# When the loads and splits of one bias matrix run, and which engine scales and shifts the first norm, in a one-layer hybrid decoder kernel

## The chip, the cores and the metric

The kernel runs as one program on one core of a Trainium2 chip. The metric is device microseconds of one execution, from launch to end. The kernel before was run three times: median 1319.92 us, from 1318.84 to 1320.48.

## The reference

One decoder layer for 256 tokens of width 1024, all in float32, with the batch of one:

```python
mod = silu(c) @ ada_w + ada_b                  # shift, scale and gate of two sub-layers
h   = rmsnorm(x, norm1_g) * (1.0 + sc1) + sh1
x   = x + g1 * hybrid_mixer(h)                 # attention and mLSTM from one projection of h
h   = rmsnorm(x, norm2_g) * (1.0 + sc2) + sh2
x   = x + g2 * routed_moe(h)                   # 4 of 32 experts per token
return rmsnorm(x, final_g)
```

`hybrid_mixer` projects h with one wide matrix, runs stick-breaking attention over 16 heads of 64 and an mLSTM over 4 heads of 256, gates the two results and projects them back. Each expert computes `clamped_swiglu(xb @ w1 + b1) @ w2 + b2`; `b1` is a 32 x 2048 matrix of biases, one row per expert. It is this `b1` that the change is about, and the line with `sh1` and `sc1`.

## The kernel before, in words

x lies transposed in SBUF, as `xT`: 128 partitions of features, eight blocks `kt` of 256 tokens. The program has four stages.

1. **Start.** Small loads, silu of c (`silr`), the mean square of x by eight matmuls against a constant matrix (`rms_T`, line 202), and from it 1/rms, `rs1`, by a Ln and an Exp on ScalarE (`rsqrt_of`, lines 223 and 224).
2. **First stage, eight blocks kt** (lines 337 to 385). For each block `start_h` loads 1 MB of `ada_w` and reduces it against `silr` on VectorE (line 187, two instructions, giving shift and scale of the block), forms `A1` (line 361), and makes h: x times rs1 (line 359), times A1 plus shift (line 362), both on VectorE; a rounded copy `hhi` on ScalarE (line 363); and the rest `hlo` on VectorE (line 364). `start_w` loads 0.9 MB of projection weights, in two pieces of 1024 and 768 columns for each partition, and splits them likewise: `yahi` or `ybhi` on ScalarE (line 347), `yalo` or `yblo` on VectorE (line 348). `start_c` issues 45 matmuls of 128x256 on TensorE (lines 375 and 378) that accumulate seven projected chunks and the two gate rows. Weights go through a ring of four wide slots, each of which holds one block's ada piece and weight piece; a slot is loaded again when both pieces are used up.
3. **The rest of the mixer** (lines 488 to 700): four chunks of attention, each in two halves (line 515 onward), with softplus and exponential work on ScalarE and VectorE between matmuls; then the mLSTM by heads (`conv`, `scores`, `read_out`, `finish`), the gates and the output projection. Each further chunk of weights is loaded (line 113), split into `whi` (ScalarE, line 238) and `wlo` (VectorE, line 240) and used by 48 matmuls (lines 274 to 276 and 303 to 305). Pieces of `ada_w` for the later shifts are reduced in between (line 187 again).
4. **Experts**: 16 pairs of experts, whose weights stream through the rings; at the start of a pair one small matmul per bank adds `b1` (line 951).

For that matmul `b1` is kept as `b1s`, three bf16 parts of the same matrix on the partitions 0 to 127. Four groups g of 512 columns are made one after the other: four loads from the POOL queue into one tile `bt` (line 476), a rounded copy on ScalarE (line 480), and twice a subtraction on VectorE (line 482) followed by a copy on ScalarE (line 483). The tile `bt` has a single buffer:

```python
def load_b1(g):
    bts[g] = mx.tile([128, 512], F32, name="bt", bufs=1)
    for i in range(4):
        nc.gpsimd.dma_start(bts[g][32 * i:32 * i + 32], a["b1"][:, 512 * g:512 * g + 512])
```

What sets the order of the work: the program is written stage by stage, but the framework arranges the instructions of each engine by priorities and estimates of its own. Each engine then runs its list strictly in that order, and so does each DMA queue (SP's for most loads, POOL's for `b1` and a few small ones). An instruction that has to wait holds everything behind it on its engine. `tc.issue_after(x)` keeps what is issued under it behind instruction x in the arranged order. The calls of `step_of_b1` stand in the loops of the attention and of the mLSTM (lines 554 and 657), with no such tie, and the arranged lists have the `b1` work much earlier, between the instructions of the first stage.

Of the kernel before, what the change touches and what calls it, by code (L numbers as in the profile page):

```python
# [13 lines left out]
F32 = mybir.dt.float32  # L14
# [4 lines left out]
AF = mybir.ActivationFunctionType  # L19
OP = mybir.AluOpType  # L20
# [3 lines left out]
T = 256  # L24
D = 1024
KT = 8
# [37 lines left out]
def body(tc, a, out):  # L64
    nc = tc.nc
    mm = nc.tensor.matmul
    act = nc.scalar.activation
# [131 lines left out]
    def mod_of(m, kt):  # L199
        return modT[:, 8 * m + kt:8 * m + kt + 1]  # L200
# [123 lines left out]
    pif = ps_m.tile([128, 512], F32, name="pm")  # L324
    first.append(ps_m.tile([128, 512], F32, name="pm").rearrange("p (n t) -> p n t", n=2))
    wf, parts = {}, {}
    order, his = [], []
    wi = mx.tile([128, KT, 64], F32, name="cv")
    nc.gpsimd.memset(wi, 0.0)
    nc.gpsimd.tensor_copy(wi[:, :, 0:4], wif[:, :, 0:4])  # L330
    nc.gpsimd.tensor_copy(wi[:, :, 32:36], wif[:, :, 4:8])
    wihi, wilo = (mx.tile([128, KT, 64], F32R, name="cs") for _ in range(2))
    with tc.issue_after(rs1_ins):
        act(wihi, wi, AF.Copy)
    tt(wilo, wi, f32(wihi), OP.subtract)

    def start_w(kt):
        w = wf[kt] = next_slot([128, 1792])
        if kt:
            nc.sync.dma_start(w, a["w_first"][kt])  # L340
        else:
            for b in (slice(0, 1024), slice(1024, 1792)):
                nc.sync.dma_start(w[:, b], a["w_first"][kt][:, b])
        hi, lo = ((yahi, yalo), (ybhi, yblo))[kt % 2]
        for b in (slice(0, 1024), slice(1024, 1792)):
            x, h, l = (t[:, b] for t in (w, hi.rearrange("p a b -> p (a b)"), lo.rearrange("p a b -> p (a b)")))
            act(h, x, AF.Copy)
            tt(l, x, f32(h), OP.subtract)
        parts[kt] = hi, lo

    def start_h(kt):
        wa = next_slot([128, 2, D])
        if 0 < kt < KT - 1:
            nc.sync.dma_start(wa, a["ada_1"][kt])
        else:
            for i in range(2):
                nc.sync.dma_start(wa[:, i], a["ada_1"][kt][:, i])
        t0 = mx.tile([128, T], F32, name="sq")
        tt(t0, xT[:, kt, :], rs1, OP.mult)
        ada(wa, 0, (kt, 8 + kt))  # L360
        stt(A1[:, kt:kt + 1], modT[:, 8 + kt:9 + kt], 1.0, col[:, C_N1 + kt:C_N1 + kt + 1], OP.add, OP.mult)
        ts(t0, t0, A1[:, kt:kt + 1], mod_of(SH1, kt), op0=OP.mult, op1=OP.add)
        his.append(act(hhi[:, kt, :], t0, AF.Copy).ins)
        tt(hlo[:, kt, :], t0, f32(hhi)[:, kt, :], OP.subtract)

    def start_c(kt):
        hi, lo = parts[kt]
# [103 lines left out]
    bts = {}  # L471

    def load_b1(g):
        bts[g] = mx.tile([128, 512], F32, name="bt", bufs=1)
        for i in range(4):
            nc.gpsimd.dma_start(bts[g][32 * i:32 * i + 32], a["b1"][:, 512 * g:512 * g + 512])

# [7 lines left out]
    def step_of_b1(g):  # L485
        if g:
            split_b1(g - 1)
        if g < 4:
            load_b1(g)

    for c in range(4):
        if c > 2:
            qs[c] = mx.tile([128, 2, T], F32, name="q")
            pq = proj_T(take(), hT)
            fetch()
            act(qs[c], pq, AF.Copy, scale=0.125)
        q = qs[c]
        if c > 1:
            pk = proj_T(take(), hT)
            fetch()  # L500
        else:
            pk = first[1 + 4 * c]
        nc.vector.tensor_copy(kp[0:64, :, 0, :], pk[0:64])
        nc.vector.tensor_copy(kp[64:128, :, 1, :], pk[64:128])
        if c > 1:
            pv = proj_N(take())
            fetch()
            v = mx.tile([128, 2, 256], F32, name="v")
            act(v, pv, AF.Copy)
        else:  # L510
            v = vs[c]
        py = ps_m.tile([128, 512], F32, name="pm").rearrange("p (n t) -> p n t", n=2)
        for n in range(2):

            z = ps_z.tile([128, 2, 512], F32, name="pz").rearrange("p a b -> p (a b)")
            for s in range(2):
                for h in range(2):
                    o = z[:, 256 * h:256 * h + 256] if s == 0 else z[:, 512 + 128 * h:640 + 128 * h]
                    mm(o, kp[:, n, h, 128 * s:128 * s + 128], q[:, n, 128 * s:], start=h == 0, stop=False,
                       skip_group_check=True)  # L520
                o = z[:, 512 * s:512 * s + 512 - 256 * s].rearrange("p (h t) -> p h t", h=2)
                mm(o[:, :, 0:128], identb, nm1[:, None, :].to_broadcast([128, 2, 128]), start=False, stop=s == 1,
                   skip_group_check=True)
            zz = z[:, 0:768]
            l = mx.tile([128, 768], F32, name="l")
            act(l, zz, AF.Abs)
            act(l, l, AF.Exp, scale=-1.0)
            act(l, l, AF.Ln, bias=1.0)
            sp = mx.tile([128, 768], F32, name="sp")
            stt(sp, zz, 0.0, l, OP.max, OP.add)  # L530
            hi = mx.tile([128, 768], F32R, name="so", bufs=1)
            lo = mx.tile([128, 768], F32R, name="sp")
            act(hi, sp, AF.Copy)
            nc.vector.tensor_tensor(lo, sp, f32(hi), OP.subtract)
            late_q = z[:, 0:512].rearrange("p (h t) -> p h t", h=2)[:, :, 128:256]
            for x in (hi, lo):
                last = x is lo
                mm(late_q, sums[:, 1], x[:, 512:768], start=False, stop=False, skip_group_check=True)
                mm(z[:, 0:512], sums[:, 0], x[:, 0:512], start=False, stop=last, skip_group_check=True)
                mm(z[:, 512:768], sums[:, 0], x[:, 512:768], start=False, stop=last, skip_group_check=True)  # L540
            e = mx.tile([128, 768], F32, name="l")
            act(e, zz, AF.Exp)
            for h in range(2):
                hs = slice(64 * (2 * n + h), 64 * (2 * n + h) + 64)
                o = py[64 * h:64 * h + 64, n, :]
                mm(o, v[:, 0, hs], e[:, 256 * h:256 * h + 256], start=True, stop=False, skip_group_check=True)
                mm(o[:, 128:256], v[:, 1, hs], e[:, 512 + 128 * h:640 + 128 * h], start=False, stop=True,
                   skip_group_check=True)
        act(yahi[:, 2 * c:2 * c + 2, :], py, AF.Copy)
        tt(yalo[:, 2 * c:2 * c + 2, :], py, f32(yahi)[:, 2 * c:2 * c + 2, :], OP.subtract)  # L550
        if c == 0:
            split_M()
        if c in {1: 0, 2: 1, 3: 2}:
            step_of_b1({1: 0, 2: 1, 3: 2}[c])
        later((0,0,1,3,)[c])


# [95 lines left out]
    for hd in range(4):  # L653
        S, so = scores(hd, *qk[hd], last)
        later((2,2,2,2,)[hd])
        if hd in {0: 3, 1: 4}:
            step_of_b1({0: 3, 1: 4}[hd])
        if hd < 3:
            qk[hd + 1] = qk_of(hd + 1)
        last = hd, read_out(hd, S), so  # L660
# [604 lines left out]
```

## Time and profile before

| what | us |
|---|---|
| median of three runs | 1319.92 |
| lowest and highest | 1318.84, 1320.48 |
| the profiled execution, device time | 1320.84 |
| its span, from first to last instruction | 1319.2 |

Busy time over the span, by engine: TensorE (PE) 1224.6 us or 93%, VectorE (DVE) 467.9 us or 35%, ScalarE (ACT) 330.8 us or 25%, GpSimd (POOL) 32.3 us or 2%. The sixteen DMA engines moved 483.41 MB, 366 GB/s on average.

To read it: the averages mix stages that have different limits, so the stages are read one by one. A row of a timeline gives the start, the duration (or, where xN is larger than one, the time that the group of N took), engine, line, operation, output and inputs; a bracket gives the idle time of the engine just ahead and what ended it. Matmuls of one engine overlap, so the pace of TensorE is the distance between two starts, not the duration of one row. PEclk or "granted clock" is the share of full speed that TensorE was given: 1.00 is 2.4 GHz, 0.50 is 1.2 GHz.

### The profile page before, as it was taken

The numbers are of one execution on the slowest core, as the hardware profiler recorded it, in microseconds if no ns is written. First come the engines' busy times: TensorE is split into PE (matmuls) and PEld (weight loads), VectorE is DVE, ScalarE is ACT, GpSimd is POOL, SyncE is SP. The second block draws the span as 40 slices with busy tenths as digits, with TensorE's granted clock in tenths as the row PEclk, the third lists the DMA queues.
The fourth block names the chain that finished last, engine by engine and source line by source line (L and its number), as shares of the span: only waits on it lengthen the run. The fifth ranks groups of instructions, "written<-read, shape, count | busy, mean of one in ns | idle before, by whom it ended". The sixth has DMA issues, their size and how long they took to land. (4 is left out here: it accounts for less than half of the span.)

```text
span 1319.2 us, 16510 instructions
## 1 busy us (share of the span) xinstructions
PE 1224.6 (93%) x6859; PEld 675.7 (51%) x6874; DVE 467.9 (35%) x923; ACT 330.8 (25%) x616; POOL 32.3 (2%) x63
## 2 busy tenths in 40 slices
PE   4989999999989999999999999989887999989887
PEld 3978999999963343344433344333333333333333
DVE  4968898786530222031211212112012112112013
ACT  3557767655521110101101011010101011010102
POOL 3100000000000000000000000000000000000002
PEclk7989999999989999998999999999999999999999
DMA  9675556496669899999999999999999999999995
GB/s 337 216 269 223 225 209 258 173 382 241 256 225 418 354 416 428 427 426 426 428 428 426 429 427 427 427 426 427 428 426 425 426 427 427 427 428 428 427 423 212
DMA packets 44989, 483.41 MB, mean 366 GB/s; under 512 B 5318, under 2 KB 6742, under 8 KB 10860
## 3 DMA queue, kind: packets, MB, share of 16 engines
q1 hardware_dynamic: 43740, 480.53, 88.0%
q0 software_dynamic: 624, 1.23, 0.3%
q8 instruction: 56, 0.92, 0.3%
q10 hardware_dynamic: 544, 0.52, 0.1%
q14 instruction: 25, 0.20, 0.0%
HBM read 481.21 MB, written 1.05 MB: 366 GB/s over the span
## 5 line engine op out<-in xcount | busy, mean ns | idle before, releaser
L823 PE MATMUL s<-w,xg 128*64 128x512 f32 x2032 | 465.2, 601 | 30.3 <-DMA w<-in_w 27.0
L823 PEld LDWEIGHTS s<-w,xg 128*64 128x64 f32 x2032 | 135.6, 137 | 298.8 <-issue 244.7
L823 PE MATMUL t<-w,whi 128*64 128x512 f32 x948 | 212.3, 596 | 11.7 <-ACT whi L874 9.6
L840 DVE SCALAR_TENSOR_TENSOR xT<-pm,modT,xT 128x256 f32<-128x256 f32 x128 | 56.0, 480 | 391.3 <-PE pm L823 391.3
L823 PEld LDWEIGHTS t<-w,whi 128*64 128x64 f32 x948 | 65.1, 137 | 137.1 <-issue 114.0
L240 DVE TENSOR_TENSOR wlo<-w,whi 128x512 fp32r<-128x512 f32 x164 | 110.1, 687 | 43.3 <-ACT whi L238 42.7
L858 ACT ACTIVATE wlo<-wlo 128x512 f32<-128x512 f32 x32 | 20.1, 629 | 417.8 <-DVE wlo L856 411.5
L238 ACT ACTIVATE whi<-w 128x512 fp32r<-128x512 f32 x162 | 100.9, 630 | 83.9 <-PE pj L275 65.9
L856 DVE TENSOR_SCALAR wlo<-s 128x512 f32<-128x512 f32 x32 | 22.1, 691 | 238.6 <-PE s L823 223.5
L274 PE MATMUL pj<-hhi,whi 128*128 128x256 f32 x368 | 105.0, 285 | 1.5 <-ACT sgate L685 1.1
L276 PE MATMUL pj<-hhi,wlo 128*128 128x256 f32 x368 | 105.1, 286 | 0.5 <-DVE wlo L240 0.5
L275 PE MATMUL pj<-hlo,whi 128*128 128x256 f32 x368 | 104.4, 284 | 0.0
L274 PEld LDWEIGHTS pj<-hhi,whi 128*128 128x128 f32 x368 | 70.5, 192 | 2.5 <-ACT sgate L685 1.3
L276 PEld LDWEIGHTS pj<-hhi,wlo 128*128 128x128 f32 x368 | 70.4, 191 | 1.5 <-DVE wlo L240 1.1
L275 PEld LDWEIGHTS pj<-hlo,whi 128*128 128x128 f32 x368 | 70.5, 191 | 0.2 <-issue 0.2
L823 PEld LDWEIGHTS pm<-G,mghi 128*128 128x128 f32 x512 | 59.5, 193 | 17.9 <-issue 17.3
L823 PE MATMUL pm<-S,whi 128*128 128x256 f32 x240 | 67.3, 404 | 0.2 <-DVE xT L840 0.2
L823 PEld LDWEIGHTS pm<-S,whi 128*128 128x128 f32 x240 | 40.8, 189 | 50.0 <-issue 34.6
L823 PE MATMUL pm<-G,mghi 128*128 128x128 f32 x512 | 63.8, 280 | 0.2 <-ACT xg L851 0.2
L187 DVE CUSTOM_DVE_ANT_0 w<-w,silr,col 128x1024 f32<-128x1024 f32 x48 | 60.3, 1279 | 1.0 <-ACT silr L673 0.5
L874 ACT ACTIVATE whi<-pm 128x512 f32<-128x512 f32 x32 | 19.1, 597 | 162.2 <-PE pm L826 162.2
L851 ACT ACTIVATE xg<-pm,modT 128x128 f32<-128x128 f32 x128 | 37.1, 368 | 69.4 <-PE pm L823 69.4
(367 smaller groups left out, 1300.9 us busy)
## 6 DMA issues: line engine op xcount, KB each, us to landing
w<-in_w SPq DMA_DIRECT2D x176, 2048.0 KB, 32.6
w<-in_w_in SPq DMA_DIRECT2D x29, 1024.0 KB, 8.1
w<-in_ada SPq DMA_DIRECT2D x22, 1024.0 KB, 7.0
w<-in_w SPq DMA_DIRECT2D x20, 1024.0 KB, 8.5
w<-in_w_first SPq DMA_DIRECT2D x7, 896.0 KB, 9.9
w<-in_w_last SPq DMA_DIRECT2D x6, 1024.0 KB, 34.4
w<-in_w_a SPq DMA_DIRECT2D x4, 1024.0 KB, 7.7
w<-in_w_b SPq DMA_DIRECT2D x4, 1024.0 KB, 13.2
```

The source lines that it names most:

```text
L187: nc.vector.tensor_tensor_reduce(out=w[:, j + n, :], in0=w[:, j + n, :], in1=SILU[-1], scale=1.0, scalar=col[:, C_AB + i:C_AB + i + 1], op ...
L238: act(hi, x, AF.Copy)
L240: nc.vector.tensor_tensor(lo, x, f32(hi), OP.subtract)
L274: mm(ps[:, n, :], whi[:, j, s], mhi[:, kt, :], start=kt + n == 0, stop=False, skip_group_check=True)
L275: mm(ps[:, n, :], whi[:, j, s], mlo[:, kt, :], start=False, stop=False, skip_group_check=True)
L276: mm(ps[:, n, :], wlo[:, j, s], mhi[:, kt, :], start=False, stop=last, skip_group_check=True)
L823: return tc.keep_in_program_order(mm(*args, **kw))
L840: stt(xT[:, kt, :], p[:, j, :], mod_of(G2, kt), xT[:, kt, :], OP.mult, OP.add)
L851: act(xg[kt] if isinstance(xg, list) else xg[:, kt, :], p[:, width * j:width * j + width], AF.Identity, bias=mod_of(SH2, kt))
L856: ts(g, glu, LIMIT, None, op0=OP.min)
L858: act(s, g, AF.Sigmoid, scale=ALPHA)
L874: act(aT[hf], pt.rearrange("p (k m) -> p k m", k=4), AF.Copy)
```

## The change

The loads and splits of `b1` are tied to the attention: in each chunk c they are kept behind the two instructions that end the chunk, step c after chunk c, and the last split (step 4) is in the first head of the mLSTM. Their tile takes a buffer of `cs` (two buffers, used also by the gate rows, by the sigmoid in `conv` and by `hn`) in place of the one of `bt`.

Scale and shift of the first norm move to ScalarE: `hhi` is written by an ACTIVATE with the scale and the shift as operands, and a second ACTIVATE of the same inputs writes the unrounded h that `hlo` needs. The VectorE instruction of line 362 is gone. x times rs1 is made for 1, 2, 3 and 2 blocks at once into tiles of the attention that are not yet in use.

Besides, the second piece of the first block's weight split is kept behind rs1 and behind the first x times rs1, and the split of the gate weights (`wihi`, `wilo`) is kept behind the first h.

```diff
+    def split_if(ins):
+        with tc.issue_after(ins):
+            act(wihi, wi, AF.Copy)
+        tt(wilo, wi, f32(wihi), OP.subtract)
...
+            if kt == 0 and b.start:
+                with tc.issue_after(rs1_ins), tc.issue_after(first_t0):
+                    act(h, x, AF.Copy)
+                    tt(l, x, f32(h), OP.subtract)
+                continue
...
+    def normed1(kt):
+        for k0, n, name, at in ((0, 1, "sp", 0), (1, 2, "sp", 1), (3, 3, "sp", 0), (6, 2, "so", 0)):
+            if k0 <= kt < k0 + n:
+                if k0 not in x1:
+                    x1[k0] = (x1[0] if at else mx.tile([128, 768], F32, name=name, bufs=2 if name == "sp" else 1)
+                              .rearrange("p (k t) -> p k t", k=3))
+                    made.append(tt(x1[k0][:, at:at + n], xT[:, k0:k0 + n],
+                                   rs1[:, None, :].to_broadcast([128, n, T]), OP.mult).ins)
+                return x1[k0], at + kt - k0
...
-        t0 = mx.tile([128, T], F32, name="sq")
-        tt(t0, xT[:, kt, :], rs1, OP.mult)
         ada(wa, 0, (kt, 8 + kt))
         stt(A1[:, kt:kt + 1], modT[:, 8 + kt:9 + kt], 1.0, col[:, C_N1 + kt:C_N1 + kt + 1], OP.add, OP.mult)
-        ts(t0, t0, A1[:, kt:kt + 1], mod_of(SH1, kt), op0=OP.mult, op1=OP.add)
-        his.append(act(hhi[:, kt, :], t0, AF.Copy).ins)
-        tt(hlo[:, kt, :], t0, f32(hhi)[:, kt, :], OP.subtract)
+        x, k = normed1(kt)
+        h = mx.tile([128, T], F32, name="sq")
+        act(hhi[:, kt, :], x[:, k, :], AF.Identity, scale=A1[:, kt:kt + 1], bias=mod_of(SH1, kt))
+        h_ins = act(h, x[:, k, :], AF.Identity, scale=A1[:, kt:kt + 1], bias=mod_of(SH1, kt)).ins
+        tt(hlo[:, kt, :], h, f32(hhi)[:, kt, :], OP.subtract)
+        if kt == 0:
+            split_if(h_ins)
+        if kt < KT - 1:
+            normed1(kt + 1)
...
-        bts[g] = mx.tile([128, 512], F32, name="bt", bufs=1)
+        bts[g] = mx.tile([128, 512], F32, name="cs")
...
-        act(yahi[:, 2 * c:2 * c + 2, :], py, AF.Copy)
-        tt(yalo[:, 2 * c:2 * c + 2, :], py, f32(yahi)[:, 2 * c:2 * c + 2, :], OP.subtract)
+        on_act = act(yahi[:, 2 * c:2 * c + 2, :], py, AF.Copy).ins
+        on_dve = tt(yalo[:, 2 * c:2 * c + 2, :], py, f32(yahi)[:, 2 * c:2 * c + 2, :], OP.subtract).ins
         if c == 0:
             split_M()
-        if c in {1: 0, 2: 1, 3: 2}:
-            step_of_b1({1: 0, 2: 1, 3: 2}[c])
+        with tc.issue_after(on_act), tc.issue_after(on_dve):
+            step_of_b1(c)
...
-        if hd in {0: 3, 1: 4}:
-            step_of_b1({0: 3, 1: 4}[hd])
+        if hd == 0:
+            step_of_b1(4)
```

What it does to the arranged lists is shown at three places. The first is ScalarE's list between the table load that precedes 1/rms and the first block of h. Before (`b1s<-bt` is a step of `b1`, `yahi<-w` a weight split, `rs` is 1/rms, `cs<-cv` the gate weights):

```order
L163 ACT_TABLE_LOAD
L480 ACTIVATE b1s<-bt 128x512
L347 ACTIVATE yahi<-w 128x1024
L223 ACTIVATE rs<-pm,epsc 128x256
L347 ACTIVATE yahi<-w 128x768
L224 ACTIVATE rs<-rs 128x256
L334 ACTIVATE cs<-cv 128x512
L483 ACTIVATE b1s<-bt 64x512
L363 ACTIVATE hhi<-sq 128x256
```

and with the change:

```order
L163 ACT_TABLE_LOAD
L353 ACTIVATE yahi<-w 128x1024
L223 ACTIVATE rs<-pm,epsc 128x256
L224 ACTIVATE rs<-rs 128x256
L350 ACTIVATE yahi<-w 128x768
L385 ACTIVATE hhi<-sp,modT,A_162 128x256
L386 ACTIVATE sq<-sp,modT,A_162 128x256
L335 ACTIVATE cs<-cv 128x512
```

The two `b1s` rows have left this stretch, and the second weight piece and the gate weights stand behind 1/rms and behind h.

The second place is VectorE's list at the end of the first stage, from the scale of the last block to the copies of k (`kp`) that the first attention matmuls read. Before:

```order
L361 SCALAR_TENSOR_TENSOR A_162<-modT,col 128x1
L406 CAST sums<-cst 128x128
L362 TENSOR_SCALAR sq<-sq,A_162,modT 128x256
L409 CAST nm<-sq 128x256
L418 COPY bf<-bif 4x1
L439 CAST neg_698<-l 68x512
L364 TENSOR_TENSOR hlo<-sq,hhi 128x256
L425 MEMSET sq 4x256
L482 TENSOR_TENSOR bt<-bt,b1s 64x512
L482 TENSOR_TENSOR bt<-bt,b1s 32x512
L503 COPY kp<-pz 64x2x256
L504 COPY kp<-pz 64x2x256
```

and with the change:

```order
L382 SCALAR_TENSOR_TENSOR A_162<-modT,col 128x1
L433 CAST sums<-cst 128x128
L445 COPY bf<-bif 4x1
L466 CAST neg_697<-l 68x512
L387 TENSOR_TENSOR hlo<-sq,hhi 128x256
L452 MEMSET sq 4x256
L530 COPY kp<-pz 64x2x256
L531 COPY kp<-pz 64x2x256
L436 CAST nm<-sq 128x256
```

The scale and shift (`sq<-sq,A`) and the two `bt` rows are gone ahead of `kp`, and the cast of the mask `nm` stands behind it.

The third place is ScalarE's list with the change, at the end of the last attention chunk (names with their numbers, so that the groups of `b1` can be told apart: `cs_866`, `cs_1372` and `cs_1092` are the groups 1, 3 and 2):

```order
L510 ACTIVATE b1s_721<-cs_866 32x512
L238 ACTIVATE whi_1528<-w_1442 128x512
L569 ACTIVATE l_1330<-pz_1307 128x768
L553 ACTIVATE l_1343<-pz_1336 128x768
L238 ACTIVATE whi_1532<-w_1442 128x512
L554 ACTIVATE l_1343<-l_1343 128x768
L238 ACTIVATE whi_1536<-w_1442 128x512
L555 ACTIVATE l_1343<-l_1343 128x768
L596 ACTIVATE xpad1_1388<-pj_1474 128x2x256
L238 ACTIVATE whi_1605<-w_1603 128x512
L507 ACTIVATE b1s_721<-cs_1372 128x512
L560 ACTIVATE so_1349<-sp_1347 128x768
```

Between the last copy of group 1 and the first copy of group 3, which takes its buffer, now stand nine rows; the four loads of group 3 can start only after that last copy, on the POOL queue, where nothing else stands ahead of them. Further on in the same list the sigmoids of the first head's q and k stand on both sides of a table load, so this head has four table loads where it had two.

## Rows read from the trace of the kernel before

**Rows 1.** Windows: stretch, length, PE, PEld, DVE, ACT, POOL busy, PEclk, DMA share, GB/s.

```profile
27.50:62.50 35.00, 35.00 (x272) 34.92 (x272) 34.70 (x63) 16.67 (x24) 3.91 (x8) 0.92 0.72 258
...
80.00:160.00 80.00, 78.31 (x576) 70.31 (x577) 67.91 (x113) 61.01 (x96) 0.00 (x0) 0.96 0.56 214
...
160.00:280.00 120.00, 117.27 (x938) 114.31 (x937) 106.69 (x215) 79.78 (x136) 3.88 (x4) 1.00 0.62 245
...
400.00:1200.00 800.00, 755.78 (x3569) 294.25 (x3584) 148.68 (x315) 91.15 (x217) 3.81 (x13) 0.99 1.00 423
```

**Rows 2.** Timeline of ScalarE, 21 to 28 us: start, time, instruction, idle ahead.

```profile
21.77 0.63 ACT L480 ACTIVATE b1s<-bt 128x512 bf16<-128x512 f32 x1 [9.52 <-DMA bt<-in_b]
...
22.31 1.04 ACT L347 ACTIVATE yahi<-w 128x1024 fp32r<-128x1024 f32 x1
...
23.26 0.46 ACT L223 ACTIVATE rs<-pm,epsc 128x256 f32<-128x256 f32 x1
...
24.35 0.40 ACT L224 ACTIVATE rs<-rs 128x256 f32<-128x256 f32 x1
...
27.03 0.42 ACT L363 ACTIVATE hhi<-sq 128x256 fp32r<-128x256 f32 x1 [1.12 <-DVE sq L362]
```

**Rows 3.** Timeline of SP's queue: issue of the first block's weight pieces.

```profile
3.49 1.00 SPq L343 DMA_DIRECT2D w<-in_w_first  x2
```

**Rows 4.** DMA issues, 0 to 80 us: count, KB each, us to landing.

```profile
w<-in_w_first SPq DMA_DIRECT2D x1, 512.0 KB, 11.4
```

**Rows 5.** Timeline of VectorE: first block's weight split and x times 1/rms.

```profile
23.38 1.22 DVE L348 TENSOR_TENSOR yalo<-w,yahi 128x1024 fp32r<-128x1024 f32 x1
...
24.78 0.43 DVE L359 TENSOR_TENSOR sq<-xT,rs 128x256 f32<-128x256 f32 x1 [0.17 <-ACT rs L224]
```

**Rows 6.** Timeline of TensorE: the first stage's first matmul.

```profile
27.50 0.58 PE L375 MATMUL pz<-hhi,yahi 128*128 128x256 f32 x1 [13.70 <-ACT hhi L363]
```

**Rows 7.** Windows of TensorE: stretch, length, busy (matmuls), PEclk, DMA share, GB/s.

```profile
28.00:30.00 2.00, 2.00 (x11) 0.50 1.00 394
```

**Rows 8.** Groups of VectorE, 27.5 to 62.5 us: count, busy us, mean ns.

```profile
L482 DVE TENSOR_TENSOR bt<-bt,b1s 32x512 f32<-32x512 f32 (+1 forms) x4 | 2.8, 689 | 0.1
...
L362 DVE TENSOR_SCALAR sq<-sq,A,modT 128x256 f32<-128x256 f32 x6 | 2.5, 413 | 0.2
```

**Rows 9.** Timeline of TensorE from the eighth block to the attention.

```profile
70.47 0.58 PE L375 MATMUL pz<-hhi,ybhi 128*128 128x256 f32 x1 [2.16 <-ACT hhi L363]
...
73.62 0.39 PE L375 MATMUL pz<-hlo,ybhi 128*128 128x256 f32 x1
73.84 0.29 PE L375 MATMUL pz<-hhi,yblo 128*128 128x256 f32 x1
73.96 0.28 PE L375 MATMUL pz<-ybhi,hlo 128*128 128x256 f32 x1
...
81.45 2.05 PE L519 MATMUL pz<-q,kp 128*128 128x256 f32 x4 [3.87 <-DVE kp L504]
...
87.42 0.40 PE L274 MATMUL pj<-hhi,whi 128*128 128x256 f32 x1
...
96.66 1.13 PE L519 MATMUL pz<-q,kp 128*128 128x256 f32 x4
...
98.21 0.36 PE L305 MATMUL pj<-whi,hlo 128*128 128x256 f32 x1
```

**Rows 10.** Timeline of ScalarE: the last step of `b1` that waits for its load.

```profile
77.13 0.63 ACT L480 ACTIVATE b1s<-bt 128x512 bf16<-128x512 f32 x1 [6.71 <-DMA bt<-in_b]
```

**Rows 11.** The tile `bt`: its loads, from issue to landing.

```profile
DMA to landing us min/median/max: 3.9/5.3/9.5
```

**Rows 12.** Timeline of ScalarE: a table load and its neighbours.

```profile
153.89 0.60 ACT L549 ACTIVATE yahi<-pm 128x512 fp32r<-128x512 f32 x1 [0.47 <-PE pm L547]
154.51 1.28 ACT L578 ACT_TABLE_LOAD   x1
155.80 0.63 ACT L578 ACTIVATE cs<-cv 128x512 f32<-128x512 f32 x1
```

More of the change, by code (lines that the diff above doesn't have):

```diff
@@ L326, in body @@
     wf, parts = {}, {}
-    order, his = [], []
+    order = []
     wi = mx.tile([128, KT, 64], F32, name="cv")
@@ L332, in body @@
     wihi, wilo = (mx.tile([128, KT, 64], F32R, name="cs") for _ in range(2))
-    with tc.issue_after(rs1_ins):
-        act(wihi, wi, AF.Copy)
-    tt(wilo, wi, f32(wihi), OP.subtract)
+    def split_if(ins):
+        with tc.issue_after(ins):
+            act(wihi, wi, AF.Copy)
+        tt(wilo, wi, f32(wihi), OP.subtract)
     def start_w(kt):
@@ L349, in start_w @@
         parts[kt] = hi, lo
+    x1 = {}
+    def normed1(kt):
[7 more added lines that the diff above has]
+                return x1[k0], at + kt - k0
+    made = []
+    normed1(0)
+    first_t0 = made[0]
     def start_h(kt):
```

## The prediction

> **What bounds the kernel now.** I read the windows first, because the averages mix stages. Of the 35 us from 27.5 on, which are six blocks of the first stage, TensorE is busy for 35.00 and VectorE for 34.70 at a granted clock of 0.92 [rows 1]: both are full. From 80 to 160 us, in the attention, TensorE has 78.31 of 80, VectorE 67.91 and ScalarE 61.01; from 160 to 280 TensorE still has 117.27 of 120. So the mixer is paced by TensorE, with VectorE close behind. In the experts (400 to 1200) the DMA share is 1.00 at 423 GB/s, while in the three mixer windows it is 0.72, 0.56 and 0.62. The experts' loads start when TensorE gives slots free in the mixer, and the DMA engines have room there, so I expect an earlier end of the mixer to pass on in full.
>
> Then the timelines, for places where TensorE does nothing. There are three. The first matmul of the stage starts at 27.50 after 13.70 us of idleness, which an `hhi` of ScalarE ends [rows 6]. The eighth block starts at 70.47 after 2.16 us, again for `hhi`, and the attention starts at 81.45 after 3.87 us, for a `kp` copy of VectorE [rows 9]. Behind each the clock is low: from 28 to 30 us it is 0.50, the lower of its two levels, 1.2 GHz, against 2.4 [rows 7]; after 70.47 the starts are 0.22 us apart (73.62 to 73.84) until they fall to 0.12 (73.84 to 73.96) [rows 9].
>
> What holds the first is in ScalarE's timeline: the first split of `b1` stands ahead of everything and waits 9.52 us for its load, until 21.77 [rows 2]. The same wait, 6.71 us until 77.13, comes back at the end of the stage [rows 10]; behind it VectorE's last steps of `b1` stand ahead of `kp`, as the second place of the arranged lists shows.
>
> **The change part by part.**
>
> *The start.* With the `b1` row gone, ScalarE's first work is the weight split. Its piece of 512 KB is issued by SP at 3.49 [rows 3] and lands 11.4 us later [rows 4], at 14.9. The mean square is no later than that: before, TensorE is done with it at 27.50 − 13.70 = 13.80 [rows 6]. Then, on ScalarE, `yahi` 1.04 (15.9), Ln 0.46 and Exp 0.40 (16.8) [rows 2]; on VectorE beside it `yalo` 1.22 (17.1), then x times 1/rms 0.43 (17.5) [rows 5]; then `hhi` 0.42 [rows 2], 18.0. The second weight piece waits on purpose until that chain is through. With a hand-over of 0.1 the first matmul starts at 18.1 instead of 27.50: **−9.4**. Bounds: a w_first load 3 us later, since loads that were spread now crowd, gives −6.4; nothing gives more than −10.
>
> *The six blocks.* VectorE loses the scale and shift, 2.5 us in six or 0.41 for each block, and the `b1` subtractions, four of 0.69 or 0.46 for each block [rows 8]. From 34.70/6 = 5.8 us a block it falls to 4.9. TensorE needs 45 matmuls at 0.12, 5.4. So TensorE becomes the slower and VectorE runs ahead of it. ScalarE gets a second copy of h per block, 0.42 to 0.60 us as the rows for 256 and 512 columns bound it [rows 2, 12]; it was busy for 16.67 of 35 [rows 1], so that costs nothing while its wait for `b1` is gone. x times 1/rms for several blocks moves the same elements in fewer instructions: nothing. The gain is at the eighth block: the idle 2.16 goes, and so do the slow matmuls between 70.47 and 73.84, some 3.37/0.22 = 15 of them at 0.10 too much, 1.5. Together **−3.7**. Lower bound 0, if the eighth block's ada load and not VectorE makes it late; upper −6, if VectorE cost further time in earlier blocks.
>
> *The gap ahead of the attention.* `kp` now follows `hlo` directly in VectorE's list. The 3.87 shrink to 0.3, about a copy's time: **−3.6**, between −2.5 and −3.9.
>
> *The first attention matmuls.* After the gap they run from 81.45 to 87.42, 5.97 us for two half chunks' worth of four; a later group of four takes 98.21 − 96.66 = 1.55 at full clock [rows 9], two of them 3.1. Without a gap the clock stays up: **−2.9**; 0 if the work then waits for other engines.
>
> *What is given back.* The `b1` work moves to where TensorE is paced by its own work, but the others are nearly full: twelve ScalarE instructions of 0.63 [rows 10], 7.5 us, and eight of VectorE of 0.69 [rows 8], 5.5 us, against 19 us that ScalarE and 12.1 that VectorE have free in the 80 us [rows 1]. The first head also gets two more table loads of 1.28 [rows 12], 2.6 us of ScalarE. If all is hidden, 0. If none of VectorE's is and the table loads show in full, 8.1; and a late group of `b1` can add to it: the load of group 3 waits for group 1's last copy, takes up to 9.5 us [rows 11], and ScalarE has nine instructions of about 0.60 [rows 12], 5.4, to fill that time, so it stands for up to 4.1. That makes 12.2 in all. I take **+3**, nearer to hidden: TensorE's idle time in that window is 1.7 of 80 with VectorE at 85%; I let it double, +1.7, and half of the table loads show, +1.3. Below 0 I see nothing, since no wait is removed there.
>
> On the table loads the Trainium skill speaks against the change: "ScalarE: Activation LUTs", section "What ACT_TABLE_LOAD costs", puts a switch at about 2.66 us, a load of 1.28 and a drain of about 1.38. The trace agrees on the load, 1.28, and shows no drain: the neighbours end at 154.49 and start at 155.80 around a load from 154.51 to 155.79 [rows 12]. By the page the two loads would be 5.3, and the sum 1.4 higher.
>
> **The sum** goes against the profiled execution, 1320.84, which is 0.92 above the median of the three: 1320.84 − 9.4 − 3.7 − 3.6 − 2.9 + 3.0 = 1304.2, and 0.92 less on the median's scale, 1303.3, rounded to **1303.0**.
>
> **The rivals.**
>
> *The attention gives back more.* The bounds above, taken together: the `b1` steps show as waits of TensorE, the last group's load holds ScalarE, and each halt is followed by matmuls at the low clock. For it: VectorE has only 12.1 us free of 80, and the steps sit at the ends of chunks, where the next chunk's weights are split. Against it: they are tied behind the chunk's own last instructions, and the scores for the next half stand ahead. A give-back of 8 to 12 makes 1308 to 1312. Chance 0.16.
>
> A rule of the Trainium skill would feed this rival: "SBUF — State Buffer", section "SBUF: two separate sides", says that a load issued by POOL waits for its descriptors while VectorE runs certain copies. The trace so far speaks against a large effect: with VectorE busy for 34.70 of 35 us [rows 1], loads of `bt` issued by POOL landed within 9.5 us at most [rows 11].
>
> *The first stage becomes bound by its loads.* A block takes 1.92 MB; at the 258 GB/s of the window [rows 1] that is 7.4 us against TensorE's 5.4. If the four blocks that have to wait for a slot of the ring came at that pace, 8 us would be lost again: about 1311. Against it: the 258 is what was asked for, not what can be had; the DMA share is 0.72, and from 28 to 30 us 394 GB/s flow [rows 7], which is 4.9 us a block. Chance 0.06.
>
> *The gain does not arrive.* The experts are bound by DMA with share 1.00 [rows 1]; if their loads start no earlier, whatever the mixer gains is a wait at the first pair: 1320, the same. Against it: DMA shares of 0.56 to 0.72 in the mixer. Chance 0.04.
>
> *Slower.* ScalarE and VectorE become the bound in the attention: in each of the eight half chunks TensorE waits and then runs at the low clock, as it did at 70.47, where a wait of 2.16 brought 1.5 of slow matmuls, 3.66 together [rows 9]. All eight would be 29.3, against 19.6 gained: about 1329. It decides from the sixth of the eight on. For it: 67.91 and 61.01 of 80 us [rows 1] get 5.5 and 10.1 us more, 92 and 89%. Against it: neither passes 100%. Chance 0.03.
>
> **How the numbers follow.** The forecast has 0.71, its own range 1299 to 1308: a give-back from 0 to 8 makes 1300.3 to 1308.3, and the upper bounds of stage and gap reach some 1.3 further down. The start's −6.4 and the stage's 0 lie within the same spread. The range for 8 in 10 takes in most of the first rival: 1298.5 to 1310.5. A measurement of this kernel can tell about 0.2%, 2.6 us, from no change. Faster by more: the forecast and the first two rivals, 0.93. Within it: 0.04. Slower: 0.03.
>
> **What would show it.** In the timeline of TensorE the first stage starts near 18 and no idle time over 0.5 us stands ahead of the eighth block or the attention, which starts near 64.7 (81.45 − 9.4 − 3.7 − 3.6), at a granted clock of 1.00. ScalarE has no wait for `b1` ahead of the first h. VectorE is under 90% busy in the first stage. From the attention's start to its end TensorE's idle time is under 4 us; if it is over 8, the first rival holds. ScalarE's row for group 3's first copy shows whether it waits for its load. If the first stage's blocks wait for `w` or `ada` loads, the second rival holds; if the first pair of experts starts as early as the mixer ends but its weights come late, the third. The prediction is wrong if the start of the attention moves by less than 15 us, or if it moves and the end doesn't.

## The result, and the profile after

With the change the kernel takes 1301.42 us (median of four runs, 1300.57 to 1303.24), against 1319.38 for the kernel before in four runs beside it. The ratio is 0.9863, with a 95% interval from 0.9847 to 0.9878: 18 us faster. The profiled execution took 1301.86 us, its span is 1300.2 against 1319.2 before. The forecast was 1303.0. One slow execution of the kernel before (2487 us) and one of the ninth kernel below (2825 us) are in no time or ratio given.

The windows of the kernel with the change, cut at stretches that answer to [rows 1] (length, busy time and number of instructions of PE, PEld, DVE, ACT and POOL, granted clock, DMA share, GB/s):

```profile
18.00:53.00 35.00, 35.00 (x276) 35.00 (x275) 33.28 (x54) 18.63 (x27) 0.00 (x0) 0.93 0.96 378
62.00:142.00 80.00, 78.68 (x603) 71.05 (x602) 72.28 (x120) 62.34 (x101) 7.88 (x16) 1.00 0.67 244
...
400.00:1200.00 800.00, 753.45 (x3565) 292.03 (x3576) 154.61 (x327) 90.57 (x214) 3.82 (x13) 1.00 1.00 423
```

The experts look as before, 423 GB/s at a DMA share of 1.00; they only begin earlier. In the attention (second row) VectorE has 4.4 us more work in 80 than it had, ScalarE 1.3. In the first stage VectorE is still busy for 33.28 of 35 us, which the prediction had not expected.

ScalarE's timeline at the start (start, time, instruction, idle time ahead) shows the wait for `b1`, 9.52 us in [rows 2], gone; it waits 1.98 us for the weights instead, and the chain down to `hhi` runs through:

```profile
13.92 1.06 ACT L353 ACTIVATE yahi<-w 128x1024 fp32r<-128x1024 f32 x1 [1.98 <-DMA w<-in_w_first]
14.88 0.46 ACT L223 ACTIVATE rs<-pm,epsc 128x256 f32<-128x256 f32 x1
15.37 0.42 ACT L224 ACTIVATE rs<-rs 128x256 f32<-128x256 f32 x1
15.69 0.83 ACT L350 ACTIVATE yahi<-w 128x768 fp32r<-128x768 f32 x1
16.60 0.60 ACT L385 ACTIVATE hhi<-sp,modT,A 128x256 fp32r<-128x256 f32 x1
```

TensorE's timeline at the places that answer to [rows 6, 9], the eighth block among them (57.85), and each later place in the mixer down to the gates where it stood idle for 0.3 us or more:

```profile
17.26 0.58 PE L402 MATMUL pz<-hhi,yahi 128*128 128x256 f32 x1 [3.33 <-ACT hhi L385]
...
57.54 0.28 PE L405 MATMUL pm<-hhi,cs 128*64 128x256 f32 x1
57.85 0.39 PE L402 MATMUL pz<-hhi,ybhi 128*128 128x256 f32 x1
...
63.35 1.02 PE L546 MATMUL pz<-q,kp 128*128 128x256 f32 x4
...
66.33 0.36 PE L274 MATMUL pj<-hhi,whi 128*128 128x256 f32 x1
...
70.25 0.19 PE L475 MATMUL pm<-cst,rows 4*128 4x4 f32 x1 [0.45 <-issue]
...
87.02 0.39 PE L274 MATMUL pj<-hhi,whi 128*128 128x256 f32 x1 [0.32 <-ACT v L536]
...
153.62 0.38 PE L274 MATMUL pj<-hhi,whi 128*128 128x256 f32 x1 [0.73 <-ACT whi L238]
...
239.85 0.33 PE L670 MATMUL pm<-cst,cs 128*128 128x128 f32 x1 [0.81 <-DVE cs L662]
246.23 0.39 PE L274 MATMUL pj<-hhi,whi 128*128 128x256 f32 x1 [1.06 <-ACT sgate L712]
```

Between the first matmul and the attention there is no bracket: TensorE stops neither ahead of the attention nor, to speak of, ahead of the eighth block, where two starts are 0.31 us apart instead of 0.12. The lead over the kernel before, point by point, with the sum of the prediction up to there:

| point | before | after | lead | forecast |
|---|---|---|---|---|
| first matmul of the first stage | 27.50 | 17.26 | 10.24 | 9.4 |
| first matmul of the attention | 81.45 | 63.35 | 18.10 | 16.7 |
| first matmul of the next weights | 87.42 | 66.33 | 21.09 | 19.6 |
| first matmul behind the gates' sigmoid | 265.17 | 246.23 | 18.94 | 16.6 |
| end of the span | 1319.2 | 1300.2 | 19.0 | 16.6 |

The lead of 18.94 at the gates arrives at the end in full. Between 66 and 246 us, 2.15 are given back, where 3 were forecast.

### The profile page after: what moved, and what is told of

Read it like the earlier page. It is cut to its first block, busy times and chain, and to the rows that moved or that the text cites. A ratio compares the mean times of both kernels' runs of the same rounds, so it can differ in the third digit from the quotient of the medians.

```text
span 1300.2 us, 16506 instructions
## 1 busy us (share of the span) xinstructions
PE 1217.3 (94%) x6859; PEld 670.4 (52%) x6874; DVE 466.2 (36%) x911; ACT 337.4 (26%) x626; POOL 32.5 (3%) x63
## 4 chain that ended last, share of the span: by engine, by line
PE 58%; DMA 35%; DVE 3%; ACT 3%; issue 1%; POOL 0%; SPq 0%; DVEq 0%; POOLq 0%; ACTq 0%
DMA w<-in_w 32%; PE s L850 19%; PE t L850 9%; PE pm L850 6%; PE pj L274 4%; PE pj L276 4%; PE pj L275 4%; DMA w<-in_w_last 2%; PE pz L402 2%; PE pm L853 1%; PE pj L402 1%; DMA w<-in_w_first 1%; PE pj L303 1%; PE pj L304 1%; PE pj L305 1%
## 6 DMA issues: line engine op xcount, KB each, us to landing
w<-in_w_first SPq DMA_DIRECT2D x7, 896.0 KB, 14.9
```

## The experiments

Twelve kernels ran. In each diff, lines that only follow from the edit are left out.

**What each part is worth: the norm alone.** The change without its `b1` part; the two ties of the first block stay in:

```diff
-        bts[g] = mx.tile([128, 512], F32, name="cs")
+        bts[g] = mx.tile([128, 512], F32, name="bt", bufs=1)
...
-        with tc.issue_after(on_act), tc.issue_after(on_dve):
-            step_of_b1(c)
+        if c in {1: 0, 2: 1, 3: 2}:
+            step_of_b1({1: 0, 2: 1, 3: 2}[c])
```

> The kernel with the change, but b1's loads and splits as before (early, in their own single buffer). Theory (the gain is b1's waits): ScalarE still waits for b1's first load, so the first stage starts near 27 us and the gap of 3 to 4 us ahead of the attention stays; only the stall ahead of the eighth block (2.16 us) and the slow matmuls behind it (1.5 us) may go, 1315 to 1320 us. Rival (the relief of VectorE is what pays): over 8 us faster than before, under 1311 us.

It took 1312.8 us, ratio 0.9947 (0.993 to 0.9964): 7 us faster, between the two expectations. Timelines of ScalarE, TensorE and VectorE of this kernel:

```profile
22.02 0.63 ACT L507 ACTIVATE b1s<-bt 128x512 bf16<-128x512 f32 x1 [10.08 <-DMA bt<-in_b]
...
26.47 0.58 PE L402 MATMUL pz<-hhi,yahi 128*128 128x256 f32 x1 [10.52 <-ACT hhi L385]
...
69.54 0.38 PE L402 MATMUL pz<-hhi,ybhi 128*128 128x256 f32 x1 [2.19 <-ACT hhi L385]
...
73.10 0.68 DVE L530 COPY kp<-pz 64x512 f32<-64x512 f32 x1 [1.93 <-ACT q L490]
...
75.39 1.02 PE L546 MATMUL pz<-q,kp 128*128 128x256 f32 x4
...
81.36 0.63 ACT L507 ACTIVATE b1s<-bt 128x512 bf16<-128x512 f32 x1 [1.74 <-DMA bt<-in_b]
```

The wait for `b1` at the start is there, as expected, and so is the stall ahead of the eighth block, for which the theory allowed either. But the gap ahead of the attention is gone (lead 81.45 − 75.39 = 6.06) although `b1` is early: in this arrangement the last group's first split comes at 81.36 us, behind the `kp` copies instead of ahead of them. So the gap came from where the arrangement put one group, and not from `b1` being early as such. Without the gap the first attention matmuls are quick too, and the lead is 9.06 at the next weights, of which 1.03 is from the start; 7.13 of it arrive at the gates. The 7 us are therefore mostly the gap's, and say little on the relief of VectorE. After the stall of 2.19 us the clock here stayed at 1.00 (69.5 to 72 us), where before it fell.

**`b1` alone.** The kernel before, with the reverse of that edit:

> The kernel before, with only b1 moved into the attention; the norm stays on VectorE. Theory: the first stage starts near 18 us, VectorE needs 5.8 - 0.46 = 5.3 us per block against TensorE's 5.4, the gap ahead of the attention goes: 1301 to 1306 us, of which at most 3.7 us are missing against the whole change. Rival (VectorE's relief by the norm pays): TensorE waits in several blocks and the time is over 1309 us.

1303.41 us, ratio 0.9878 (0.9861 to 0.9894): 16 of the 18 us. There is no stall ahead of the eighth block and no gap ahead of the attention. The start is at 19.93 us instead of 17.26, because the second weight piece stands ahead of 1/rms and the gate weights ahead of the first h:

```profile
19.93 0.58 PE L375 MATMUL pz<-hhi,yahi 128*128 128x256 f32 x1 [4.42 <-ACT hhi L363]
```

So the two parts make 7 and 16 alone and 18 together: the traces of both lack the gap ahead of the attention with its low-clock matmuls, and it can go only once.

**The first wait alone.** All splits of `b1` in the kernel before are kept behind the first `hhi`:

```diff
-        act(b, bt, AF.Copy)
-        for lo in (64, 96):
+        with tc.issue_after(his[0]):
+            act(b, bt, AF.Copy)
+        for lo in (64, 96):
```

> The kernel before, with all steps of b1's splits kept behind the first block's hhi, and otherwise where they were. This takes away the wait at the start alone. Theory: the first stage starts near 18 us, 9.4 us earlier; the wait for the last b1 load ahead of the attention stays, 2 to 4 us, and low-clock matmuls behind it: 1306 to 1312 us. Rival (the terms are one: whatever is gained at the start is lost again, because the wait for b1's loads only moves): 1316 us or more.

1306.32 us, ratio 0.9897 (0.9881 to 0.9914), at the near end of the theory's range. The start came at 20.13 us, a lead of 7.37, and a stall of 2.04 us ahead of the eighth block stayed. The expected gap ahead of the attention did not: with the splits arranged anew it is gone, as with the norm alone. So one tie brings thirteen of the 18 us, but not by the first wait alone: the lead grows to 12.61 at the attention and 15.60 at the next weights because the gap and its low-clock matmuls went too.

**The price of `b1` in the attention.** The change, with all steps of `b1` left out:

```diff
+    nc.gpsimd.memset(b1s, 0.0)
...
-        with tc.issue_after(on_act), tc.issue_after(on_dve):
-            step_of_b1(c)
...
-        if hd == 0:
-            step_of_b1(4)
```

> The kernel with the change, with the loads and splits of b1 left out (b1s is set to zero once, so the experts' biases b1 are missing). It prices b1's work in its new place. Theory (mostly hidden): 0 to 2 us faster than the change, 1299.5 to 1301.5 us. Rival (the work of b1 shows in the attention): 3 us or more faster, under 1298.5 us.

1299.69 us, ratio 0.985 (0.9833 to 0.9866): 1.7 us under the change, as expected, though the intervals of the two overlap. The trace is clearer. Its lead at the first matmul of the next weights is 20.69 and at the gates 20.76, so nothing is given back, against 2.15 with `b1`. The arranged list of this kernel has four table loads in the first head too, so those cost nothing that shows.

The trace also shows what holds the first stage. Here the clock was 1.00 from the first matmul on (17.65 us), TensorE was through the first seven blocks sooner, and a stall stands ahead of the eighth, although neither `b1` nor the norm's scale and shift burdens VectorE:

```profile
58.25 0.39 PE L402 MATMUL pz<-hhi,ybhi 128*128 128x256 f32 x1 [1.44 <-ACT hhi L385]
```

**The start, by the ties.** `b1` moved and the two ties of the first block, with the norm left on VectorE:

```diff
+            if kt == 0 and b.start:
+                with tc.issue_after(rs1_ins), tc.issue_after(t0s[0]):
+                    act(h, x, AF.Copy)
+                    tt(l, x, f32(h), OP.subtract)
+                continue
...
+        if kt == 0:
+            split_if(his[0])
```

> The kernel before, with b1 moved into the attention and the two ties of the first block (second weight piece behind 1/rms and behind the first x times 1/rms; gate weights behind the first h). The norm's scale and shift stays on VectorE. Theory A (what b1's move alone lacked, 2.0 us, is the start: there the first matmul came at 19.93 us against 17.26): start near 17.3 us, 1301 to 1302.5 us, like the whole change, so that scale and shift on ScalarE is worth nothing measurable. Theory B (VectorE's relief by the norm is the missing 2 us): 1303 us or more though the start is early, with TensorE waiting for VectorE in the first stage.

1302.79 us, ratio 0.9878 (0.9861 to 0.9894): by time it is not told apart from either neighbour, and it lies between the two theories. In TensorE's timeline the start is early, the clock is high at once, and the time is lost again ahead of the eighth block:

```profile
17.99 0.39 PE L383 MATMUL pz<-hhi,yahi 128*128 128x256 f32 x1 [2.15 <-ACT hhi L369]
...
58.50 0.38 PE L383 MATMUL pz<-hhi,ybhi 128*128 128x256 f32 x1 [1.38 <-ACT hhi L369]
```

That looks like theory B, but it is not: the kernel just before has the norm on ScalarE, the same high clock and the same stall, 1.44 us. VectorE's timelines of the change and then of this kernel, at the first reduction of the second and of the seventh block, five blocks apart:

```profile
18.89 1.28 DVE L187 CUSTOM_DVE_ANT_0 w<-w,silr,col 128x1024 f32<-128x1024 f32 x1
...
46.91 1.28 DVE L187 CUSTOM_DVE_ANT_0 w<-w,silr,col 128x1024 f32<-128x1024 f32 x1
```

```profile
19.20 1.28 DVE L187 CUSTOM_DVE_ANT_0 w<-w,silr,col 128x1024 f32<-128x1024 f32 x1
...
47.22 1.28 DVE L187 CUSTOM_DVE_ANT_0 w<-w,silr,col 128x1024 f32<-128x1024 f32 x1
```

Both take 28.02 us, 5.60 a block. Moving scale and shift to ScalarE did not make VectorE any faster. The stall depends on how early TensorE arrives.

The windows of TensorE from 18 to 20 us of this kernel, then of the change (matmuls, clock, DMA share, GB/s):

```profile
18.00:20.00 2.00, 2.00 (x17) 1.00 0.97 403
```

```profile
18.00:20.00 2.00, 2.00 (x12) 0.50 1.02 422
```

**An earlier start, and a warm one.** Three kernels on top of the change: Ln and Exp ahead of the first weight split; nine idle matmuls instead of two ahead of the stage; both.

```diff
+            if kt == 0:
+                with tc.issue_after(rs1_ins):
+                    act(h, x, AF.Copy)
```

```diff
-            warm(2)
+            warm(9 if name == "rs" else 2)
```

> The kernel with the change, with Ln and Exp of 1/rms ahead of the first weight split on ScalarE. The weights land at 13.9 us, the mean square is done near 13.5, so x times 1/rms and the first split can overlap. Theory (the start is now a chain of ScalarE, 0.46 + 0.42 us of which move in front of the wait for the weights): first matmul near 16.4 us, 0.5 to 1 us faster, 1300.4 to 1301 us. Rival (the start is set by the weights' landing, or the low clock takes it back): no earlier start, 1301.4 us.

1301.33 us, ratio 0.9858 (0.9841 to 0.9874): no gain. TensorE started at 16.47, as expected, and then stood still for 1.19 us until 18.16, for `yalo`; the attention began at 63.4 as in the change.

> The kernel with the change, with nine instead of two idle matmuls on TensorE between the mean square and the first stage, so that it doesn't stand still for 3.3 us there. Theory (the first stage is paced by TensorE, and from 17.3 to 23 us by its low clock, 0.21 us for a matmul against 0.12): the clock is high from the first matmul or soon after, 2 to 3 us faster, 1298.5 to 1299.5 us. Rival (the first stage is bound by its loads, DMA share 0.96 there): TensorE then waits for w or ada in the first blocks and the time stays at 1301 us.

1302.04 us, ratio 0.9865 (0.9848 to 0.9881): no gain. The clock was not high from the first matmul: 0.59 and 0.56 from 18 to 22 us, and 1.00 from 22 to 24, where the change had 0.72. A stall of 1.10 us stood ahead of the eighth block.

> Both of the two before together. Theory: the gains add, 2.5 to 4 us faster than the change, 1297.5 to 1299 us. Rival (loads bound the first stage): 1301 us; and if the idle matmuls end later than the first h is ready, a later start of up to 1 us.

1302.4 us, ratio 0.9872 (0.9855 to 0.9888): no gain by time. In its trace the clock was high, and the attention began at 62.7, 0.6 earlier than with the change, after three stalls of 0.57 to 1.12 us in the first two blocks and one of 0.27 ahead of the eighth.

In time all three came out near what their rivals said, but not for the rivals' reason. In the waits of the first stage of the change (17 to 58 us) VectorE waits for ScalarE only, and ScalarE has 2.3 us for `w` in two early blocks:

```profile
DVE yalo L354 <- ACT yahi L353: 0.9, 3, 0.3
DVE yblo L354 <- ACT ybhi L353: 0.6, 2, 0.3
...
ACT ybhi L353 <- DMA w<-in_w_first: 1.4, 1, 1.4
ACT yahi L353 <- DMA w<-in_w_first: 0.9, 1, 0.9
```

VectorE's timeline of one block of the change shows what sets the pace:

```profile
35.99 1.28 DVE L187 CUSTOM_DVE_ANT_0 w<-w,silr,col 128x1024 f32<-128x1024 f32 x1
...
38.40 0.08 DVE L187 DVE_READ_ACCUMULATOR2_ANT modT<- 128x1 f32 x1
38.52 0.16 DVE L382 SCALAR_TENSOR_TENSOR A<-modT,col 128x1 f32<-128x1 f32 x1
...
39.84 0.42 DVE L387 TENSOR_TENSOR hlo<-sq,hhi 128x256 fp32r<-128x256 f32 x1
40.57 0.96 DVE L354 TENSOR_TENSOR yalo<-w,yahi 128x768 fp32r<-128x768 f32 x1 [0.31 <-ACT yahi L353]
41.45 1.28 DVE L187 CUSTOM_DVE_ANT_0 w<-w,silr,col 128x1024 f32<-128x1024 f32 x1
```

A block takes 41.45 − 35.99 = 5.46 us, and TensorE needs 5.4. The 0.31 is a loop between two engines: VectorE makes A, ScalarE makes `hhi` and h from it and only then splits the second weight piece, for which VectorE waits. ScalarE's timeline of the same block, and its `hhi` of the eighth:

```profile
38.71 0.60 ACT L385 ACTIVATE hhi<-sp,modT,A 128x256 fp32r<-128x256 f32 x1 [2.68 <-DVE A L382]
...
39.71 0.83 ACT L353 ACTIVATE yahi<-w 128x768 fp32r<-128x768 f32 x1
...
57.20 0.60 ACT L385 ACTIVATE hhi<-so,modT,A 128x256 fp32r<-128x256 f32 x1 [4.05 <-DVE A L382]
```

An earlier or warmer TensorE runs into this pace. The change itself is already at it: its eighth `hhi` is ready at 57.80, and TensorE takes it at 57.85. In the three kernels the eighth block begins at 57.92, 58.43 and 57.22, though they start at 16.47, 17.84 and 15.85.

**The loop broken.** The weight piece is split ahead of h on ScalarE, in the blocks 1 to 6, by keeping `hhi` behind it:

```diff
+        with tc.issue_after(his[kt]) if 0 < kt < KT - 1 else contextlib.nullcontext():
+            act(hhi[:, kt, :], x[:, k, :], AF.Identity, scale=A1[:, kt:kt + 1], bias=mod_of(SH1, kt))
...
+            his[kt] = act(h, x, AF.Copy).ins
```

> The kernel with the change, with the second weight piece of the blocks 1 to 6 split ahead of the block's h on ScalarE. With the change, ScalarE splits it behind h, and VectorE waits for it 0.31 us in a block and 0.12 for other hand-overs, so that it needs 5.46 us for a block, as much as TensorE. Theory (VectorE sets when the eighth block is ready, at 57 to 58.5 us in every variant so far, whatever the start or the clock): VectorE needs 5.1 to 5.2 us for a block, the eighth h is ready 1.5 to 2 us sooner, but TensorE, at the low clock until 23 us, can't use it: 1300.5 to 1301.5 us. Rival (the loads set it): VectorE's pace stays at 5.4 us and it waits for w or ada.

VectorE's timeline of this kernel, one block:

```profile
39.51 1.28 DVE L188 CUSTOM_DVE_ANT_0 w<-w,silr,col 128x1024 f32<-128x1024 f32 x1
...
42.15 2.10 DVE L355 TENSOR_TENSOR yblo<-w,ybhi 128x1024 fp32r<-128x1024 f32 x2
...
44.50 1.28 DVE L188 CUSTOM_DVE_ANT_0 w<-w,silr,col 128x1024 f32<-128x1024 f32 x1
```

The block takes 44.50 − 39.51 = 4.99 us, with no wait for a load: the theory holds for VectorE, and more than expected. The ratio is 0.9859 (0.9841 to 0.9878), not told apart from the change. In the profiled execution (1299.15 us) the clock was high from the first matmul, which had not been expected, and the attention began at 61.1. The other executions took 1301.34 and 1302.08, so this one was the best of three.

With nine idle matmuls as well, and then also with Ln and Exp first:

> The one before, with nine idle matmuls ahead of the first stage instead of two. Theory (VectorE bound the first stage, so only both together pay): no stall ahead of the eighth block although TensorE starts warm for some matmuls, 0.5 to 2 us faster than the change, 1299.5 to 1301 us. Rival (loads): the stall of about 1 us ahead of the eighth block stays, 1302 us.

1300.28 us (1299.87 to 1300.74), ratio 0.9848 (0.9834 to 0.9862): the best of those that compute everything. There is no stall ahead of the eighth block any more, which the theory asked for. Against the change it is 1.1 us by the medians; the intervals overlap, so a gain is likely and not shown.

> The one before, and Ln and Exp of 1/rms ahead of the first weight split. Where TensorE then starts near 15.9 us at the high clock at once, VectorE is late for the first two blocks. Theory (VectorE): the stalls sum to 1 to 2 us in the first blocks and none stands ahead of the eighth; the attention starts near 61.5 us against 63.35; 1299 to 1300 us. Rival (loads): the attention starts at 62.7 us as without the new order of the splits.

1300.72 us, ratio 0.9855 (0.9839 to 0.987). The start came at 16.04, with a stall of 1.41 us for `yalo` behind it and none ahead of the eighth block. The attention began at 62.6, the time of the rival, but for another reason: the clock was 0.57 from 18 to 20 us, where it had been expected high.

**`b1` still later.** The nine-matmul kernel, with the steps in the chunks 2 and 3 and the heads 0 to 2, and their tile in a buffer of its own again:

```diff
+        if c > 1:
+            with tc.issue_after(on_act), tc.issue_after(on_dve):
+                step_of_b1(c - 2)
...
+        if hd < 3:
+            with tc.issue_after(s_ins[hd]):
+                step_of_b1(hd + 2)
```

> The kernel with the new order of the splits and nine idle matmuls, with the b1 steps two places later (chunks 2 and 3, heads 0 to 2) and their tile in a buffer of its own, as before the change. Leaving the b1 work out took 2.15 us of give-back away, from 20.7 us of lead after the first matmuls of the attention to 20.8 at its end. Theory (it is ScalarE and VectorE in the attention that are short of time): later steps cost less, 0.5 to 2 us faster than the same kernel without it. Rival (the cost is in the number of steps and table loads, wherever they stand): no difference within 0.5 us, or slower, as VectorE is 90% busy from 140 to 260 us.

1304.5 us, ratio 0.9878 (0.9862 to 0.9894): 4 us slower than without it. The theory fails; the rival had allowed for a slower kernel, without a size. TensorE waits 4.00 us at the gates, where it waited 1.06:

```profile
248.42 0.58 PE L275 MATMUL pj<-hhi,whi 128*128 128x256 f32 x1 [4.00 <-ACT sgate L725]
```

From 225 us to the gates ScalarE has three table loads ahead of the one for `sgate` (229.06, 231.37, 233.27), where the kernel without the edit has one (230.93), and `sgate` starts at 247.77 instead of 244.82. Whether it is the later steps or the new arrangement with its table loads that costs the time was not taken apart.

## Why the prediction was right, and where its steps were off

**The start** (−9.4) measured −10.24, past the −10 that was called the most. The chain is the one predicted; `w_first` was split from 13.92 on where 14.9 was taken, which gives most of the difference, and `hhi` took 0.60 where 0.42 was taken. The first-tie kernel shows that the wait for `b1` held the start: with only that wait gone the lead there is 7.37, and with `b1` moved and the two ties it is 9.51.

**The blocks and the gap** (−3.7 and −3.6, 7.3 together) measured 7.86 together, from the start's lead of 10.24 to 18.10: 2.38 up to the eighth block's first matmul (70.47 before, 57.85 now), 1.61 within that block, and the gap's 3.87. The sum was right, but three of its reasons were not.

First, VectorE was to fall from 5.8 to 4.9 us a block and run ahead of TensorE. The 5.8 took the 35 us of [rows 1] for six blocks; VectorE's timeline before shows five from the second block's reduction to the seventh's in 30.39 us, 6.08 each:

```profile
27.25 1.28 DVE L187 CUSTOM_DVE_ANT_0 w<-w,silr,col 128x1024 f32<-128x1024 f32 x1
...
57.64 1.28 DVE L187 CUSTOM_DVE_ANT_0 w<-w,silr,col 128x1024 f32<-128x1024 f32 x1
```

It fell to 5.60, and the norm's move has no part in that, since the kernel with the norm on VectorE has 5.60 too. The prediction took the instructions out and left the hand-overs at nothing. Scale and shift left VectorE, and x times 1/rms for the later blocks is done in two of the earlier ones; in exchange VectorE waits in the later blocks, 0.12 us ahead of A and 0.31 for the weight piece that ScalarE splits behind h. The one cancels the other. What made VectorE faster is `b1`'s subtractions leaving: three stood in those 30.39 us, 0.72 each from start to start. By time the norm's move is not shown to be worth anything either: 1302.79 against 1301.42, with intervals that overlap. The sign "VectorE under 90% busy in the first stage" was wrong, 95%.

Second, the stall ahead of the eighth block was to go because TensorE becomes the slower engine. What the runs show is that it went because `b1`'s subtractions left and because TensorE, at a clock of 0.50 until about 23 us, reached that block just when its `hhi` was ready. In three kernels with `b1` out of the first stage where the clock rose earlier, the stall was 1.44 us (no `b1`), 1.38 (`b1` and the ties) and 1.10 (nine idle matmuls), with the norm on either engine. That part of the sum came out by luck: the low clock at the start, which the prediction did not count on, cost the change nothing that shows, for TensorE would have waited.

Third, the gap of 3.87 belonged to one group's place in the list; every new arrangement removed it, with `b1` early as well.

**The first attention matmuls** (−2.9) measured 21.09 − 18.10 = −2.99.

**The give-back** (+3) measured 2.15. It was the `b1` work, since without it nothing was given back; the 1.3 put down for table loads did not show. By the Trainium skill, "ScalarE: Activation LUTs", section "What ACT_TABLE_LOAD costs", the sum would have been an estimated 1.4 higher; the kernel without `b1`, with four loads in the first head, showed no cost of them at all. The rule of the Trainium skill in "SBUF — State Buffer", section "SBUF: two separate sides", that a load issued by POOL can be held up by VectorE's copies, cost nothing here: group 3 was issued by POOL at 129.65, and its first copy at 141.16 did not wait.

**The rivals.** More given back in the attention did not come: 2.15 is far under its 8 to 12, and group 3's load was not late. That the first stage becomes bound by its loads came nearer than thought: the DMA share rose from 0.72 to 0.96, at 378 GB/s, and still VectorE never waited for a load. The passage through the experts was whole, 18.94 to 19.0. The slower case had its price too high as well: a stall of 2.19 us does not always bring the low clock.

## What to carry to other kernels

An instruction that waits for a load is paid by everything behind it on its engine, so what is needed last should be kept back by a tie, also when it looks free. When work moves from a full engine to an idle one, count the new hand-overs: here they ate all of what left VectorE. And before speeding up the engine that looks busiest, take the pace of the one that feeds it: three kernels with an earlier or warmer TensorE gained nothing that shows in the time while VectorE stood at 5.46 us a block.

## What was not expected of the hardware

The granted clock at the beginning of the first stage does not follow from the idle time ahead of it alone. After 3.33 us of idleness it was 0.50 with the change; after 3.07 us, with the same work ahead, it was 1.00 in the kernel with the loop broken. With nine idle matmuls and only 2.33 us of idleness it began high and fell while TensorE was busy. The first matmul and a window of TensorE of the kernel with the loop broken, then windows of the kernel with nine idle matmuls:

```profile
16.80 0.39 PE L406 MATMUL pz<-hhi,yahi 128*128 128x256 f32 x1 [3.07 <-ACT hhi L389]
...
18.00:20.00 2.00, 2.00 (x19) 1.00 1.01 418
```

```profile
18.00:20.00 2.00, 2.00 (x13) 1.92 (x13) 2.00 (x4) 0.67 (x2) 0.00 (x0) 0.74 1.02 423
20.00:22.00 2.00, 2.00 (x12) 2.00 (x11) 2.00 (x5) 1.79 (x2) 0.00 (x0) 0.50 1.00 412
```

What decides it stays open; each of these is one profiled execution.
